# Seven products in six of eight up blocks, and thirteen whole units

## The chip, the core and the metric

The kernel runs on one core of a Trainium2 chip. TensorE (PE) multiplies, VectorE (DVE) and ScalarE (ACT) convert, scale and add, GpSimd (POOL) does a little elementwise work, and SyncE (SP) issues the loads. Each engine runs its own instructions in order, and semaphores tie them together. The metric is the time of one execution on the device in microseconds (us).

## The reference

A decoder trunk of two layers over 256 rows of 2048 columns, in float32. Each layer has an attention (differential in layer 0, latent in layer 1), a cross attention to 256 memory rows, and an MLP; each is normed before and added to the stream after. The change lies in the MLP:

```python
def sq_relu_mlp(h, wup, wdown):
    return jnp.square(jax.nn.relu(h @ wup)) @ wdown

x = x + sq_relu_mlp(rms_norm(x, mlp_norm[i]), mlp_wup[i], mlp_wdown[i])
```

with `wup` of 2048 x 8192 and `wdown` of 8192 x 2048 in each layer.

## The kernel before

**A product in three.** The kernel keeps float32 accuracy with operands of a shorter kind: every operand is held as a high half (rounded, type fp32r) and a low half (what rounding left), and one product is three matmuls, high by high, high by low, low by high. The activations are the stationary operand, 128x128, and the weights the moving one, 512 columns.

**A tile of weights.** `fetch` and `split_weights` load 1 MB of weights, 128 x 2048, into one of six tiles of the pool `wraw` (`raw`, line 168). `halves_of` makes from it two half tiles: for each, ScalarE casts 1024 columns into `whi` (line 193) and VectorE subtracts that from the raw tile into `wlo` (line 194). The pool `whalf` has four buffers of each, which is two tiles. `fill` keeps four tiles (`AHEAD`) prepared in the program's order ahead of the one that `take` hands to TensorE.

**The MLP in blocks.** The 8192 hidden columns are eight blocks of 1024. An *up block* multiplies the normed stream by one block of `wup`; its relu, squared and transposed, is kept in two *hidden units*, `hid[b, c]`, one for each half of 512 columns. A *down* group multiplies hidden units by the rows of `wdown` that belong to them, in four chunks of 512 output columns, and each chunk ends with two additions to the stream, one for each 128 rows (`add_residual`, line 428). An ordinary tile is one *item* of a line: 24 matmuls, for two row tiles.

**Seven products.** For the blocks in `SEVEN` the class `Seven` cuts the product of activations (2 x 2 parts: row tile by half of the inner dimension) and weights (2 x 2 parts) in the manner of Strassen and Winograd: seven products of sums and differences in place of eight. Each product takes two tiles (`x` 0 and 1) of 12 matmuls each into one bank, named `pr`, so a block has 14 items. The sums of the activations (`s1` to `s4`) are made once a layer. The sums of the weights are made for each block by VectorE in place, on whole raw tiles: for `p5` (line 735), `p7` (740), `p6` (743) and `p4` (748), each out of a newly loaded tile and a tile that is still kept, or of two kept ones. Twelve tiles are loaded for a block, where an ordinary block loads eight. `products` then adds the seven results: `p1` and `p5` are copied out of their banks by ScalarE (line 780), and after `p6`, `p2` and `p4` seven additions on VectorE (line 775) give the four quarters of the block. `out` takes each: relu and square on ScalarE (lines 1026 and 1027), transposes on TensorE (line 162), and a split into halves (lines 282 and 283).

**The order.** `mlp_line` writes out the order of items by hand. Before, it starts with up block 0, and then each of the blocks 1, 3, 5 and 7 is spread over the ordinary items of one group: the down group of the blocks that wait, and the next even up block. At the end comes the down group of block 7 alone. TensorE's instructions keep the program's order. Those of the other engines are put in order by a scheduler that runs its own picture of the time. A transpose is placed in TensorE's order when a running count of time in the program (`clock`) has passed the wait that its task named: `T_SQ + 2.0`, 6.4 us, for the results of the seven products.

**Units.** The pool `units` has twelve tiles of 8 KB in each partition, and beside them two half units of 4 KB, which the latent attention uses for its rotated queries. In the MLP, eight units hold the activations and their sums, and the others are hidden units.

Of the kernel before, what the change touches and what calls it, by code (L numbers as in the profile page):

```python
# [11 lines left out]
F32R = mybir.dt.float32r  # L12
# [5 lines left out]
P = 128  # L18
D = 2048
S = 256  # L20
NT = 2
CH = 512
# [1 line left out]
WARM = 16  # L24
RAWS = 6
MLP_BLOCKS = 8
SEVEN = (1, 3, 5, 7)
EVS = 7

T_EV, T_TURN, T_ROT, T_SM, T_SQ, T_ADD, T_NORM = 2.6, 2.6, 9.0, 6.5, 4.4, 2.2, 4.5  # L30
# [15 lines left out]
def trunk(ctx, tc, x, xT, mem, memT, positions, gcols, gfinal, lam_vecs, consts, W, out):  # L46
    nc = tc.nc

    def pool(name, bufs, space=None):
        kw = {"space": space} if space else {}  # L50
        return ctx.enter_context(tc.tile_pool(name=name, bufs=bufs, **kw))
# [1 line left out]
    keep = pool("keep", 1)  # L53
    wraw = pool("wraw", RAWS)
    whalf = pool("whalf", 4)
    units = pool("units", 12)
    work = pool("work", 2)
    small = pool("small", 3)
    banks = pool("banks", 8, bass.MemoryType.PSUM)
# [3 lines left out]
    def nm(s):  # L63
        serial[0] += 1
        return f"{s}_{serial[0]}"

    def unit():
        return units.tile([P, 2, 4, S], F32R, tag="unit", name=nm("unit"))

    def half_unit():  # L70
        return units.tile([P, 2, 2, S], F32R, tag="half", name=nm("half"), bufs=2)

    def bank(tag="ax"):
        return banks.tile([P, CH], F32, tag="bank", name=nm(tag))
# [7 lines left out]
    class Task:  # L82
        def __init__(self, gen):
            self.gen = gen
            self.done = False
            self.waits = None
            self.ready = clock[0]
            self.serial = serial[0]
            side.append(self)
            self.step()  # L90
# [36 lines left out]
    class Held:  # L127
# [6 lines left out]
        def run(self, gen):  # L134
            self.tasks.append(Task(gen))
            return self
# [7 lines left out]
    def side_bank():  # L144
        while not free_banks[0]:
            yield 0.5
        free_banks[0] -= 1
        return bank()

    def give_back():  # L150
        free_banks[0] += 1
# [45 lines left out]
    plan = []  # L197
# [492 lines left out]
        plan_k(f"ca_wo{l}", 4)  # L690

    def plan_mlp(l):
        plan.extend(j for item in mlp_lines[l] for j in item.jobs)

    class Chunk:


        def __init__(self, l, kind, blocks, c):
            self.kind, self.blocks, self.c = kind, blocks, c
            if kind == "up":  # L700
                self.all = [(f"mlp_wup{l}", 4 * (2 * blocks[0] + c) + u, CH) for u in range(4)]
            else:
                self.all = [(f"mlp_wdown{l}", 8 * b + 2 * c + u, CH) for b in blocks for u in range(2)]

        def items(self):
            return [Item(self, u, [job]) for u, job in enumerate(self.all)]
# [89 lines left out]
                out(1, 0, c["u3"])  # L796

    def mlp_line(l):
        def up(b):
            return [i for c in range(2) for i in Chunk(l, "up", [b], c).items()]  # L800

        def down(blocks):
            return [i for c in range(4) for i in Chunk(l, "down", blocks, c).items()]

        line = up(0)
        waiting = [0]
        for b in SEVEN:
            rest = down(waiting) + (up(b + 1) if b < 7 else [])
            seven = Seven(l, b).items()
            i = 0  # L810
            for k, item in enumerate(rest):
                while i < len(seven) and i * (len(rest) - 3) / len(seven) <= k:
                    line.append(seven[i])
                    i += 1
                line.append(item)
            waiting = [b, b + 1] if b < 7 else [b]
        return line + down(waiting)

    mlp_lines = {l: mlp_line(l) for l in range(2)}

# [113 lines left out]
    def keep2(rs, scale, tag):  # L934
        o = []
        for t in range(NT):
            k = small.tile([P, 1], F32, tag=tag, name=nm(tag), bufs=4)
            nc.vector.tensor_scalar(k, rs[t], scale, None, ALU.mult)
            o.append(k)
        return o  # L940
# [70 lines left out]
    def mlp(l, norm, gnext):  # L1011
        a = norm.done()
        rstd = keep2(norm.rstd, 1.0, "r1")
        hid = {}

        chunk = {}
        copied = {}

        def out(b, c, t, src, r, wait):

            if (b, c) not in hid:
                hid[b, c] = Held(unit())
            dst = hid[b, c]

            def task():
                nc.scalar.activation(r, src, AF.Relu, scale=rstd[t])
                nc.scalar.activation(r, r, AF.Square)
                yield wait
                pt = yield from side_bank()
                split(dst, t, transpose4(r, pt))  # L1030
                yield T_TURN
                give_back()

            dst.run(task())

        def finish_chunk(of, ps, nxt):
            for t in range(NT):
                if of.kind == "up":
                    r = work.tile([P, CH], F32, tag="ev", name=nm("ev"), bufs=EVS)
                    out(of.blocks[0], of.c, t, ps[t], r, T_SQ)  # L1040
                else:
                    add_residual(t, of.c, ps[t])
                    if nxt is not None:
                        nxt(of.c, t, ps[t])

        def acts_of(of):
            if of.kind == "up":
                return [a.unit_of(u) for u in range(4)]
            return [hid[b, c] for b in of.blocks for c in range(2)]

        def run(line, nxt=None):
            for item in line:
                of = item.of
                if isinstance(of, Seven):
                    of.products(
                        a, item.u, copied,
                        lambda t, c, r, b=of.b: out(b, c, t, r, r, T_SQ + 2.0),
                    )
                    continue
                n = len(of.all)  # L1060
                if nxt is not None and of.c == 3:
                    if item.u == 0:
                        finish_chunk(of, matmul_chunk(acts_of(of), turns=True), nxt)
                    continue
                if item.u == 0:
                    chunk["ps"] = [bank("mm") for _ in range(NT)]
                    chunk["acts"] = acts_of(of)
                act = chunk["acts"][item.u]
                need(act.tasks)
                for h, (hi, lo) in enumerate(take()):  # L1070
                    for t in range(NT):
                        unit_part(chunk["ps"][t], act, h, hi, lo, t, item.u == 0, item.u == n - 1)
                if item.u == n - 1:
                    finish_chunk(of, chunk["ps"], nxt)

        line = mlp_lines[l]
        tail = sum(len(i.of.all) == 2 and i.of.kind == "down" and i.of.blocks == [7] for i in line if not isinstance(i.of, Seven))
        limit = free_banks[0] - 1
        free_banks[0] -= limit
        run(line[:-tail])  # L1080

        def last(nxt):
            free_banks[0] += limit
            run(line[-tail:], nxt)

        if gnext is None:
            return last
        nxt = Stream(gnext)
        last(nxt.feed)
        return nxt  # L1090
# [31 lines left out]
    )  # L1122
    norm = cross(0, norm, m, mk)
    norm = mlp(0, norm, G_ATTN + 16)


# [32 lines left out]
    ps = matmul_chunk(acts, LAT)  # L1159
    latent_piece(eq, 0, ps, 0, LAT)  # L1160
    ps = matmul_chunk(acts, LAT)
# [4 lines left out]
    ps = matmul_chunk(acts, 320)  # L1166
# [24 lines left out]
        yield T_TURN  # L1191

    def project_latent(gi):
        qr, q, k, v = Held(half_unit()), Held(unit()), Held(unit()), unit()
        ps = matmul_chunk([cq], 256)

        def rotated(ps):
            es = []
            for t in range(NT):
                e = evacuate(ps[t][:, :256], rq[t])  # L1200
                rope(e[:, :256].rearrange("p (h d) -> p h d", h=4), cos[:, t, hd:], sin[:, t, hd:], 4, hm)
                es.append(e)
            yield T_ROT
            b = yield from side_bank()
            for t in range(NT):
                pt = b[:, 2 * t * P : 2 * (t + 1) * P]
                for i in range(2):
                    flip(pt[:, i * P : (i + 1) * P], es[t][:, i * P : (i + 1) * P])
            for t in range(NT):
                split(qr, t, b[:, 2 * t * P : 2 * (t + 1) * P].rearrange("p (k t) -> p k t", k=2))  # L1210
            give_back()
            yield T_TURN

        qr.run(rotated(ps))
        ps = matmul_chunk([cq])
        if gi == 0:
            krope.run(shared_key())
        for t in range(NT):
            heads_T(ps[t], t, rq[t], q, spare=True)
        ps = matmul_chunk([ckv])  # L1220
        for t in range(NT):
            heads_T(ps[t], t, rkv[t], k, spare=True)
        ps = matmul_chunk([ckv])
        for t in range(NT):
            values(ps[t], t, rkv[t], v)
        return qr, q, k, v
# [13 lines left out]
    down = mlp(1, norm, None)  # L1240
# [112 lines left out]
```

## Time and profile before

| | |
|---|---|
| median of 3 runs | 2284.94 us (2284.89 to 2284.94) |
| the profiled execution | 2284.52 us |
| its span, first to last instruction | 2282.7 us |
| granted TensorE clock, mean | 0.996 |
| TensorE busy | 2255.7 us, 99% |
| VectorE busy | 1609.0 us, 70% |
| ScalarE busy | 1281.1 us, 56% |
| 16 DMA engines busy, queue of SyncE | 56.9% |

A row of a group names line, engine, operation, output and inputs by the program's names, shape and count, then busy time, the mean of one in ns, the idle time ahead, and who ended it. A row of the timeline has start, length, engine, line and operation, and in brackets the wait ahead of it. `raw<-raw,raw` is a combination of weights, `wlo<-raw,whi` a split of half a tile. A matmul's listed length overlaps the next one.

### The profile page before, as it was taken

The numbers are of one execution on the slowest core, as the hardware profiler recorded it, in microseconds if no ns is written. First come the engines' busy times: TensorE is split into PE (matmuls) and PEld (weight loads), VectorE is DVE, ScalarE is ACT, GpSimd is POOL, SyncE is SP. The second block draws the span as 40 slices with busy tenths as digits, with TensorE's granted clock in tenths as the row PEclk, the third lists the DMA queues.
The fourth block names the chain that finished last, engine by engine and source line by source line (L and its number), as shares of the span: only waits on it lengthen the run. The fifth ranks groups of instructions, "written<-read, shape, count | busy, mean of one in ns | idle before, by whom it ended". The sixth has DMA issues, their size and how long they took to land.

```text
span 2282.7 us, 27403 instructions
## 1 busy us (share of the span) xinstructions
PE 2255.7 (99%) x10668; PEld 1884.4 (83%) x10668; DVE 1609.0 (70%) x1766; ACT 1281.1 (56%) x1731; POOL 103.4 (5%) x194
## 2 busy tenths in 40 slices
PE   8999999999999999999999999999999999999998
PEld 6888888888888888888889888888888888888886
DVE  5556657677877776777865666778787776777775
ACT  6554545566565465465555655566556546546564
POOL 0010110000000000000000311000000000000001
PEclk9999999999999999999999999999999999999999
DMA  9355555436666666666655344643766666666672
GB/s 358 121 175 187 196 203 190 166 124 226 234 228 229 220 209 226 224 204 237 223 178 174 124 142 148 240 148 129 255 243 204 220 221 221 221 221 209 233 258 74
DMA packets 69826, 458.90 MB, mean 201 GB/s; under 512 B 8001, under 2 KB 8129, under 8 KB 16961
## 3 DMA queue, kind: packets, MB, share of 16 engines
q1 hardware_dynamic: 69120, 456.12, 56.9%
q8 instruction: 83, 1.36, 0.2%
q10 hardware_dynamic: 576, 1.05, 0.2%
q14 instruction: 47, 0.38, 0.0%
HBM read 455.04 MB, written 2.10 MB: 200 GB/s over the span
## 4 chain that ended last, share of the span: by engine, by line
PE 96%; ACT 1%; DVE 1%; DMA 1%; POOL 0%; issue 0%; ACTq 0%; POOLq 0%; SPq 0%
PE mm L158 77%; PE pr L158 13%; PE ax L158 3%; PE ax L162 2%; PE mm L162 1%; ACT whi L193 1%; DMA raw<-in_da_wqkv_dram 0%; DVE wlo L194 0%; DMA raw<-in_memT_dram 0%; POOL rope L444 0%; POOL ev L449 0%; ACT junk L311 0%; ACT ev L433 0%; ACT p L490 0%; POOL rope L447 0%
## 5 line engine op out<-in xcount | busy, mean ns | idle before, releaser
L158 PE MATMUL mm<-whi,unit 128*128 128x512 f32 (+1 forms) x5312 | 1679.7, 389 | 1.4 <-ACT unit L561 0.9
L194 DVE TENSOR_TENSOR wlo<-raw,whi 128x1024 fp32r<-128x1024 f32 (+2 forms) x890 | 1071.6, 1212 | 560.1 <-ACT whi L193 541.1
L193 ACT CAST whi<-raw 128x1024 fp32r<-128x1024 f32 (+2 forms) x890 | 926.1, 1041 | 850.8 <-PE mm L158 763.2
L158 PEld LDWEIGHTS mm<-whi,unit 128*128 128x128 f32 x5312 | 994.5, 188 | 198.2 <-ACT unit L561 1.3
L158 PE MATMUL mm<-wlo,unit 128*128 128x512 f32 (+1 forms) x2656 | 1026.1, 386 | 0.8 <-DVE wlo L194 0.8
L158 PEld LDWEIGHTS mm<-wlo,unit 128*128 128x128 f32 x2656 | 500.3, 188 | 95.6 <-DVE wlo L194 1.4
L158 PE MATMUL pr<-whi,unit 128*128 128x512 f32 x896 | 298.0, 391 | 0.0
L158 PEld LDWEIGHTS pr<-whi,unit 128*128 128x128 f32 x896 | 168.3, 188 | 34.6
L158 PE MATMUL pr<-wlo,unit 128*128 128x512 f32 x448 | 174.4, 389 | 0.0
L428 DVE TENSOR_TENSOR x<-x,mm 128x512 f32<-128x512 f32 x160 | 105.2, 681 | 7.7 <-PE mm L158 6.7
L158 PEld LDWEIGHTS pr<-wlo,unit 128*128 128x128 f32 x448 | 84.1, 188 | 16.9
L317 POOL TENSOR_TENSOR rs<-rs,mhalf 128x1 f32<-128x1 f32 (+1 forms) x28 | 23.6, 846 | 1278.8 <-DVE rs L316 1278.8
L283 DVE TENSOR_TENSOR unit<-ax,unit 128x512 fp32r<-128x512 f32 x80 | 54.0, 684 | 1.1
L282 ACT CAST unit<-ax 128x512 fp32r<-128x512 f32 x80 | 45.6, 581 | 13.4 <-PE ax L162 13.4
L490 ACT ACTIVATE p<-ax,nmax 128x256 f32<-128x256 f32 (+1 forms) x80 | 33.6, 427 | 27.2 <-DVE nmax L488 26.1
L743 DVE TENSOR_TENSOR raw<-raw,raw 128x2048 f32<-128x2048 f32 x16 | 36.6, 2290 | 10.0 <-DMA raw<-in_mlp_wup_dram 9.8
L311 ACT ACTIVATE junk<-x 128x512 bf16<-128x512 f32 x56 | 35.2, 628 | 9.4 <-DVE x L428 8.4
L1251 POOL TENSOR_TENSOR x<-x,unit 128x512 f32<-128x512 f32 x6 | 8.9, 1502 | 668.2 <-ACT junk L311 668.2
L735 DVE TENSOR_TENSOR raw<-raw,raw 128x2048 f32<-128x2048 f32 x16 | 36.6, 2286 | 3.3 <-DMA raw<-in_mlp_wup_dram 2.6
L740 DVE TENSOR_TENSOR raw<-raw,raw 128x2048 f32<-128x2048 f32 x16 | 36.6, 2288 | 3.2 <-DMA raw<-in_mlp_wup_dram 3.0
L158 PE MATMUL ax<-unit,unit 128*128 128x256 f32 (+1 forms) x240 | 37.2, 281 | 0.0
L748 DVE TENSOR_TENSOR raw<-raw,raw 128x2048 f32<-128x2048 f32 x16 | 36.7, 2292 | 0.5
(148 smaller groups left out, 1009.7 us busy)
## 6 DMA issues: line engine op xcount, KB each, us to landing
raw<-in_mlp_wup_dram SPq DMA_DIRECT2D x160, 1024.0 KB, 5.0
raw<-in_mlp_wdown_dram SPq DMA_DIRECT2D x128, 1024.0 KB, 4.9
raw<-in_da_wqkv_dram SPq DMA_DIRECT2D x47, 1024.0 KB, 5.0
raw<-in_da_wo_dram SPq DMA_DIRECT2D x16, 1024.0 KB, 4.9
raw<-in_ca_wkv_dram SPq DMA_DIRECT2D x16, 1024.0 KB, 5.0
raw<-in_mla_wo_dram SPq DMA_DIRECT2D x16, 1024.0 KB, 5.1
raw<-in_ca_wq_dram SPq DMA_DIRECT2D x8, 1024.0 KB, 4.9
raw<-in_ca_wo_dram SPq DMA_DIRECT2D x8, 1024.0 KB, 4.9
```

Source lines behind the costliest of these rows:

```text
L158: return nc.tensor.matmul(o, stationary, moving, start=start, stop=stop)
L162: nc.tensor.transpose(o, src, ident)
L193: nc.scalar.copy(hi, r)
L194: nc.vector.tensor_tensor(lo, r, f32(hi), ALU.subtract)
L282: nc.scalar.copy(hi, src)
L283: nc.vector.tensor_tensor(dst[:, 1, :n, t * P : (t + 1) * P], src, f32(hi), ALU.subtract)
L311: nc.scalar.activation(junk[:, : src.shape[1]], src, AF.Square, accum_out=acc)
L428: nc.vector.tensor_tensor(xc, xc, ps, ALU.add)
L735: nc.vector.tensor_tensor(o, o, r.pop("11"), ALU.subtract)
L740: nc.vector.tensor_tensor(o, r.pop("22"), o, ALU.subtract)
L743: nc.vector.tensor_tensor(o, r.pop("t3"), o, ALU.add)
L748: nc.vector.tensor_tensor(o, o, r.pop("21"), ALU.subtract)
```

## The change

Six of the eight up blocks of a layer, 1, 2, 3, 5, 6 and 7, are multiplied by seven products, in place of 1, 3, 5 and 7. The ordinary up blocks are 0 and 4. Block 0 comes first as before. All other ordinary items but the last down group form one list, in which block 4 comes in two halves of 512 columns, (4, 0) and (4, 1), each of which joins the down group of a block ahead of it: the down groups are 0; 1 with (4, 0); 2; 3 with (4, 1); 5; 6; and 7 at the end. Over this list the 84 items of the six blocks are spread evenly. A `Chunk` is therefore given pairs of block and half in place of blocks, and `mlp_line` returns the line and its end. The pool has 13 units, and the rotated queries use half of a whole unit.

```diff
-SEVEN = (1, 3, 5, 7)
+SEVEN = (1, 2, 3, 5, 6, 7)
...
-    units = pool("units", 12)
+    units = pool("units", 13)
...
-    def half_unit():
-        return units.tile([P, 2, 2, S], F32R, tag="half", name=nm("half"), bufs=2)
...
     def plan_mlp(l):
-        plan.extend(j for item in mlp_lines[l] for j in item.jobs)
+        plan.extend(j for line in mlp_lines[l] for item in line for j in item.jobs)
...
-        def __init__(self, l, kind, blocks, c):
-            self.kind, self.blocks, self.c = kind, blocks, c
+        def __init__(self, l, kind, halves, c=0):
+            self.kind, self.halves, self.c = kind, halves, c
             if kind == "up":
-                self.all = [(f"mlp_wup{l}", 4 * (2 * blocks[0] + c) + u, CH) for u in range(4)]
+                ((b, h),) = halves
+                self.all = [(f"mlp_wup{l}", 4 * (2 * b + h) + u, CH) for u in range(4)]
             else:
-                self.all = [(f"mlp_wdown{l}", 8 * b + 2 * c + u, CH) for b in blocks for u in range(2)]
+                self.all = [(f"mlp_wdown{l}", 8 * b + 2 * c + h, CH) for b, h in halves]
...
     def mlp_line(l):
-        def up(b):
-            return [i for c in range(2) for i in Chunk(l, "up", [b], c).items()]
-
-        def down(blocks):
-            return [i for c in range(4) for i in Chunk(l, "down", blocks, c).items()]
-
-        line = up(0)
-        waiting = [0]
-        for b in SEVEN:
-            rest = down(waiting) + (up(b + 1) if b < 7 else [])
-            seven = Seven(l, b).items()
-            i = 0
-            for k, item in enumerate(rest):
-                while i < len(seven) and i * (len(rest) - 3) / len(seven) <= k:
-                    line.append(seven[i])
-                    i += 1
-                line.append(item)
-            waiting = [b, b + 1] if b < 7 else [b]
-        return line + down(waiting)
+        def up(b, h):
+            return Chunk(l, "up", [(b, h)]).items()
+
+        def down(*halves):
+            return [i for c in range(4) for i in Chunk(l, "down", halves, c).items()]
+
+        def both(b):
+            return (b, 0), (b, 1)
+
+        line = up(0, 0) + up(0, 1)
+        rest = (
+            down(*both(0)) + up(4, 0) + down(*both(1), (4, 0)) + down(*both(2))
+            + up(4, 1) + down(*both(3), (4, 1)) + down(*both(5)) + down(*both(6))
+        )
+        seven = [i for b in SEVEN for i in Seven(l, b).items()]
+        i = 0
+        for k, item in enumerate(rest):
+            while i < len(seven) and i * (len(rest) - 3) / len(seven) <= k:
+                line.append(seven[i])
+                i += 1
+            line.append(item)
+        return line, down(*both(7))
...
-            return [hid[b, c] for b in of.blocks for c in range(2)]
+            return [hid[k] for k in of.halves]
...
-        qr, q, k, v = Held(half_unit()), Held(unit()), Held(unit()), unit()
+        qr, q, k, v = Held(unit()[:, :, :2]), Held(unit()), Held(unit()), unit()
```

The lines after the change are up to ten lower or higher by number: the combinations are 733, 738, 741 and 746, the split 191, the load 165, the residual addition 425.

More of the change, by code (lines that the diff above doesn't have):

```diff
@@ L1039, in finish_chunk @@
                     r = work.tile([P, CH], F32, tag="ev", name=nm("ev"), bufs=EVS)
-                    out(of.blocks[0], of.c, t, ps[t], r, T_SQ)
+                    out(*of.halves[0], t, ps[t], r, T_SQ)
                 else:
@@ L1074, in run @@
                     finish_chunk(of, chunk["ps"], nxt)
-        line = mlp_lines[l]
-        tail = sum(len(i.of.all) == 2 and i.of.kind == "down" and i.of.blocks == [7] for i in line if not isinstance(i.of, Seven))
+        line, end = mlp_lines[l]
         limit = free_banks[0] - 1
         free_banks[0] -= limit
-        run(line[:-tail])
+        run(line)
         def last(nxt):
             free_banks[0] += limit
-            run(line[-tail:], nxt)
+            run(end, nxt)
         if gnext is None:
```

## The prediction

> **What bounds the kernel now.** I read the page's busy shares first, then the chain that ended last, then TensorE's waits, and then the two stretches in which blocks are multiplied by seven products, because the shares are an average over stages.
>
> ```profile
> span 2282.7 us, 27403 instructions
> PE 2255.7 (99%) x10668; PEld 1884.4 (83%) x10668; DVE 1609.0 (70%) x1766; ACT 1281.1 (56%) x1731; POOL 103.4 (5%) x194
> ...
> PE 96%; ACT 1%; DVE 1%; DMA 1%; POOL 0%; issue 0%; ACTq 0%; POOLq 0%; SPq 0%
> ...
> 714.56 10.88 PE mm L158 x48
> ```
>
> The chain is TensorE from end to end. In it 48 matmuls of 128x512 take 10.88 us, so one costs 0.2267 us when nothing holds it up. The 389 ns of the group list is a length that overlaps the next one.
>
> ```profile
> 559.00:1145.00 586.00, 585.34 (x2638) 484.24 (x2637) 438.74 (x382) 330.88 (x360) 0.00 (x0) 1.00 0.64 224
> 1645.00:2230.00 585.00, 584.34 (x2630) 483.18 (x2629) 434.81 (x380) 328.01 (x356) 0.00 (x0) 1.00 0.64 224
> 576.00:658.00 82.00, 82.00 (x363) 67.90 (x362) 67.67 (x59) 44.33 (x44) 0.00 (x0) 1.00 0.65 231
> ```
>
> The columns are the length, then the busy time of PE, PEld, DVE, ACT and POOL, the clock, the DMA share and GB/s. The first two rows are the seven-product stages of the two layers, the third is the densest piece of the first, with one item of the seven products to one ordinary item. TensorE never rests; VectorE is busy 75% of a stage, 83% of the dense piece.
>
> ```profile
> PE ax L162 <- ACT u L1027: 1.3, 2, 0.7
> ...
> DVE wlo L194 <- ACT whi L193: 129.4, 114, 1.5
> ACT whi L193 <- PE mm L158: 211.4, 137, 1.7
> DVE raw L743 <- DMA raw<-in_mlp_wup_dram: 5.5, 4, 2.1
> ```
>
> Waits in all, their number, the longest. The first row is of the whole run and is TensorE's only wait within these stages; the rest are of the first stage. VectorE's idle time is mostly back pressure: four buffers of split weights (two tiles) are full, ScalarE waits for TensorE to empty one, VectorE for ScalarE. A little of it is not: a combination of weights that stands waiting for its load.
>
> **The change, part by part.** *Fewer matmuls.* An ordinary block costs 2 column halves x 4 units x 24 = 192 matmuls, a block by seven products 7 x 2 x 12 = 168. Four more blocks in the two layers go over: 4 x 24 = 96 fewer, which the program's own order confirms (10,668 to 10,572). 96 x 0.2267 = 21.8 us, 10.9 a layer, all on the chain. A stage shrinks from 586 to 575.1 us.
>
> *More for VectorE.* Per layer: 24 more half-tile splits (12 tiles), 16 combinations, 14 additions of products, and 16 residual additions, since the order has seven down groups of four chunks in place of five. Their prices:
>
> ```profile
> 633.54 5.76 DVE L194 TENSOR_TENSOR wlo<-raw,whi 128x1024 fp32r<-128x1024 f32 x5
> ...
> 545.64 2.29 DVE L735 TENSOR_TENSOR raw<-raw,raw 128x2048 f32<-128x2048 f32 x1 [0.70 <-DVE unit L283]
> 547.85 1.22 DVE L194 TENSOR_TENSOR wlo<-raw,whi 128x1024 fp32r<-128x1024 f32 x1
> ...
> 576.12 1.28 DVE L428 TENSOR_TENSOR x<-x,mm 128x512 f32<-128x512 f32 x2
> ```
>
> Back to back a split costs 5.76 / 5 = 1.15, a combination 547.85 - 545.64 = 2.21, a 512-column addition 0.64. So 24 x 1.15 + 16 x 2.21 + 30 x 0.64 = 82.2 us a layer, and VectorE has 438.7 + 82.2 = 520.9 us in 575.1: 91%. Its cover is TensorE, with 54 us left a layer.
>
> *More for ScalarE:* 24 casts and 4 copies of products.
>
> ```profile
> L193 ACT CAST whi<-raw 128x1024 fp32r<-128x1024 f32 x266 | 280.4, 1054 | 246.4 <-PE mm L158 211.4 <-PE pr L158 27.4 <-DVE wlo L194 7.0
> L780 ACT COPY p<-pr 128x512 f32<-128x512 f32 x8 | 4.6, 574 | 0.0
> ```
>
> 24 x 1.054 + 4 x 0.574 = 27.6, and 358 of 575 us is 62%: hidden.
>
> *More loads.* 12 a block in place of 8, so 8 more of 1 MB a layer; 224 GB/s become about 243, and bytes do not bind (the page's first slice moved 358 GB/s). What binds is when a load can start. All six raw tiles are always taken, so each load waits for the VectorE instruction that frees one.
>
> ```profile
> DMA to landing us min/median/max: 4.7/5.0/7.4
> ...
> 624.43 0.33 SPq L168 DMA_DIRECT2D raw<-in_mlp_wup_dram  x1
> ...
> 631.33 2.29 DVE L743 TENSOR_TENSOR raw<-raw,raw 128x2048 f32<-128x2048 f32 x1 [2.09 <-DMA raw<-in_mlp_wup_dram]
> 633.54 2.35 DVE L194 TENSOR_TENSOR wlo<-raw,whi 128x1024 fp32r<-128x1024 f32 x2
> 635.11 0.39 PE L158 MATMUL pr<-wlo,unit 128*128 128x512 f32 x1
> ```
>
> The first row is of the first stage's loads of up weights. The others are one wait: the load starts at 624.43, VectorE stands 2.09 us until 631.33, and the split behind the combination (an earlier tile's; it only stands behind it in the queue) ends at 633.54 + 1.22 = 634.76. TensorE takes it at 635.11, 0.35 us later. The kernel before is this near its edge. In the instruction order of both programs I added up VectorE's work between the instruction that frees a raw tile and the combination that reads the new load. Before, 48 of 96 such loads in the two layers have under 5.0 us of work to hide in, together 43.0 us short per layer; after, 52 of 144, together 32.0. The new order is longer, not tighter, because more of VectorE's work lies between; but before, the shortfall fell into 147 us of idle time per layer, and now into 54.
>
> *Bursts.* At the end of a block the product additions crowd in. VectorE's order there (W split of half a tile, C combination, a product addition, s split of activations):
>
> ```
> before: a W a a W a a W a W s W s W W s W a
> after:  a W a W a C W a a W s a W W s W W s a
> ```
>
> Both hold 8 W, four tiles, for which TensorE has 2 x 5.44 + 2 x 2.72 = 16.3 us of matmuls (24 and 12 x 0.2267) and about 1.6 of transposes. VectorE needs 8 x 1.15 + 10 x 0.64 = 15.6 before and 2.2 more, 17.8, after. A lead lost ahead of this piece isn't won back in it.
>
> To price lateness I carried these sums along VectorE's order, TensorE at its unstalled pace: a split not before the half four ahead is used up and ScalarE's 1.05 us are over, a combination not before its load landed. The order before then has no split late, as in the trace. The new one has splits late at six or seven places a layer: 3.2 us in all with landings of 5.0, 4.7 with 5.2, 10.9 with 5.6. Each lateness may also shift what follows and so help the next place; the largest alone is 1.8. I take 4.7, since the rows have a tail (7.4) behind the median; the ends are 1.8 and 10.9.
>
> *Transposes behind the additions.* TensorE's order puts the first transposes of a finished block 30 matmuls, 6.8 us, after the sixth product, as before.
>
> ```profile
> 816.10 0.68 DVE L775 TENSOR_TENSOR u<-pr,p 128x512 f32<-128x512 f32 x1
> ...
> 818.55 0.69 DVE L775 TENSOR_TENSOR u<-pr,p 128x512 f32<-128x512 f32 x1
> ...
> 820.04 0.63 ACT L1027 ACTIVATE u<-u 128x512 f32<-128x512 f32 x1
> ...
> 821.84 0.60 PE L162 MATMUL ax<-identr,u 128*128 128x128 f32 x4
> ```
>
> ScalarE is done at 820.67, 1.17 us early, after three additions with one split among them. In the new order four of six blocks a layer have two splits there: 1.15 more, margin nil; the sixth block has two residual additions besides, 1.28 late; a combination ahead of the second output costs up to 1.2 in two blocks. Together 0 to 5 us a layer, and partly the same lateness as above; I take 2.5.
>
> *Units.* Thirteen units and no half units fill the same memory. Beside eight units of activations and their sums, five are left, and the new order never holds more than five hidden units. Outside the MLP the engines' orders are unchanged, and no unit's first write waits for TensorE beyond its own transposes: nothing, either way.
>
> *The sum.* The profiled execution took 2284.52 us, 0.42 under the median of the runs, 2284.94. 2284.94 - 21.8 + 2 x (4.7 + 2.5) = 2277.5.
>
> *A rule weighed.* Five splits in a row take 5.76 us, 1.15 each, where the list has 1.22 to 1.23 for one: the end of one overlaps the start of the next. The Trainium skill, "VectorE: DVE Perf Modes", section on the TRN2 errata, says that a fixed latency is paid between instructions, and that an fp32 tensor_tensor takes (N+151)/0.96 ns, 1224 for a split. This trace agrees with the length of one and not with paying all of it in a row. By the page's formula VectorE's stage would come to an estimated 554 us in place of 521, and the kernel to about the time before (the third rival has the same mechanism from rows).
>
> **The rivals.** *Nothing stalls* (2263 to 2267): VectorE's 521 us fit into 575 and the order spreads them. For it: no late split before, and fewer short loads per combination. Against it: margins of 0.35 and 1.17 that the bursts use up. 0.15.
>
> *Slower, by the raw tiles.* VectorE waits behind a combination whose load has just started, loses its lead of two tiles, and TensorE stops at most blocks. With landings of 6.0 my sums make 19.4 us late a layer, and with 2.5 for transposes 21.9: 2284.9 - 21.8 + 43.8 = 2307. It decides from 13.2 us of stops a layer (10.9 and half of 4.6), which landings of about 5.7 bring. Against it the median of 5.0; for it the 2.09 us wait. Most of this case would lie near 2292. 0.21.
>
> *VectorE is the bound.* If its instructions overlapped no longer once it is nearly full, a stage would cost their listed lengths: 296 splits x 1.22 + 48 combinations x 2.29 + 118 additions x 0.68 = 551 us, and with the 32 of waits 583, 8 more than TensorE's 575. That leaves 2.9 of the 10.9, and with 2.5 for transposes 0.4 a layer: 2284. Against it the five splits in a row. 0.07.
>
> *The clock falls.* A stop of 7 us early in the run shows what a long one costs:
>
> ```profile
> 54.20:58.00 3.80, 3.11 (x11) 2.52 (x12) 0.92 (x2) 1.17 (x2) 1.67 (x6) 0.50 0.01 2
> 58.00:62.00 4.00, 4.00 (x14) 3.18 (x14) 0.47 (x1) 0.59 (x1) 0.00 (x0) 0.72 0.02 4
> ```
>
> 3.8 x 0.5 + 4.0 x 0.28 = 3.0 us more per such stop. My stops are under 2 us, so this comes only with the slower rival. The Trainium skill, "TensorE: Matmul & The Clock Gate", section "HAM oscillation", puts the limit at idle gaps of about 3.4 us; these rows agree that 7 us is beyond it, and none here shows a gap near the limit. 0.02 by itself.
>
> *The change does nothing* has no place: the matmuls are gone from the order.
>
> **How the numbers follow.** My forecast, part of the saving kept, has 0.55 with 2267 to 2283 as its own range. Under 0.2% (4.6 us) a measurement of this kernel tells little from no change: below 2280.4 is faster, above 2289.5 slower. Faster is nine tenths of my case and the first rival, 0.50 + 0.15 = 0.65; same is the rest of mine, the third rival and the fourth, 0.14; slower 0.21. The range leaves out the far end of the slower rival and the lowest of the first: 2264 to 2292.
>
> **What would show it.** Right: the seven-product stages near 575 us plus 3 to 11 each, VectorE near 521 us in each, TensorE waits of 0.2 to 2 us for splits and for the transposes' inputs, most of them at block ends, attention unchanged. Wrong: TensorE waits of over 3 us, a clock under 1.00 in the stages, or landings of over 5.5 us at the combinations; or no waits at all.

## The result, and the profile after

The changed kernel takes 2296.84 us (median of four runs, 2294.0 to 2302.2) against 2284.91 of the kernel before beside it: ratio 1.0056, 95% interval 1.004 to 1.0072. It is slower by 0.56%; 2277.5 was forecast, and the range ended at 2292. The profiled execution is the longest of the four, 2302.2 us with a span of 2300.4; that of before had 2284.52 and 2282.7. So the profile has 17.7 us to explain where the medians differ by 11.9. The mean granted clock of the four runs was 0.992, 0.993, 0.995 and 0.995 at 2302.2, 2299.2, 2294.4 and 2294.0 us, so the profiled run is also the one that lost most by the clock.

The page of the changed kernel, its span, the busy shares and the engines' shares of the chain that ended last:

```profile
span 2300.4 us, 27468 instructions
PE 2248.5 (98%) x10572; PEld 1871.0 (81%) x10572; DVE 1760.1 (77%) x1906; ACT 1337.6 (58%) x1787; POOL 103.4 (4%) x194
...
PE 87%; DVE 6%; DMA 2%; ACT 2%; issue 2%; POOL 0%; ACTq 0%; POOLq 0%; SPq 0%; DVEq 0%
```

The 96 matmuls are gone, and TensorE no longer carries 96% of the chain but 87%; VectorE, ScalarE and loads stand in it. Where that happens is read from the first and last product matmul of each layer's stage, first after, then before:

```profile
L155 PE MATMUL pr<-whi,unit x672: 388/389/776, 559.9 to 1154.4; 128*128 128x512 f32 x168
...
L155 PE MATMUL pr<-whi,unit x672: 388/389/775, 1638.1 to 2230.8; 128*128 128x512 f32 x168
```

```profile
L158 PE MATMUL pr<-whi,unit x448: 388/389/481, 559.1 to 1144.9; 128*128 128x512 f32 x150
...
L158 PE MATMUL pr<-whi,unit x448: 388/389/481, 1627.0 to 2213.1; 128*128 128x512 f32 x150
```

The stages last 594.5 and 592.7 us in place of 585.8 and 586.1: 8.7 and 6.6 more, where 10.9 less was due from the matmuls. The other 2.4 lie outside the stages. Of the same two stretches that the prediction shows of before (PE, PEld, DVE, ACT and POOL busy, clock, DMA share, GB/s), the changed kernel has

```profile
559.00:1145.00 586.00, 571.74 (x2551) 469.60 (x2550) 508.76 (x446) 353.45 (x381) 0.00 (x0) 1.00 0.66 237
1645.00:2230.00 585.00, 572.65 (x2553) 470.24 (x2552) 506.66 (x446) 352.66 (x380) 0.00 (x0) 0.99 0.65 236
```

TensorE stands still for 14 and 12 us in each, with VectorE at 87%: it has 77 us left over and is late all the same. What TensorE waits for in the first stage and then in the second (us in all, times, longest):

```profile
PE ax L159 <- ACT u L1031: 8.7, 4, 2.7
PE pr L155 <- DVE wlo L191: 3.2, 4, 1.7
PE mm L155 <- DVE wlo L191: 1.7, 1, 1.7
PE ax L159 <- ACT p L1031: 0.7, 2, 0.4
```

```profile
PE ax L159 <- ACT u L1031: 8.7, 4, 2.7
PE mm L155 <- DVE wlo L191: 2.1, 2, 1.7
PE pr L155 <- DVE wlo L191: 1.1, 2, 0.7
PE ax L159 <- ACT p L1031: 0.3, 1, 0.3
```

VectorE's own waits for loads, whole run:

```profile
DVE raw L741 <- DMA raw<-in_mlp_wup_dram: 18.6, 14, 2.2
DVE raw L738 <- DMA raw<-in_mlp_wup_dram: 11.1, 8, 2.0
DVE raw L733 <- DMA raw<-in_mlp_wup_dram: 4.5, 5, 1.5
```

They add up to 34 us; in the kernel before such waits are 15.4 us in the whole run. Of TensorE's waits, the first rows are the transposes of a finished block's output: before, this wait was 1.3 us in the whole run. The end of block 1 shows where it comes from. First the kernel before, in a block of its first stage: the last matmul of the sixth product and what VectorE runs next.

```profile
814.81 0.39 PE L158 MATMUL pr<-whi,unit 128*128 128x512 f32 x1
...
813.60 2.59 DVE L194 TENSOR_TENSOR wlo<-raw,whi 128x1024 fp32r<-128x1024 f32 x2 [0.75 <-ACT whi L193]
```

The product ends at 815.20, and VectorE begins with the additions at 816.10, 0.90 later. In the changed kernel, from the timeline (start, length, engine, instruction, in brackets the wait ahead of it):

```profile
639.79 0.39 PE L155 MATMUL pr<-whi,unit 128*128 128x512 f32 x1
...
649.40 0.66 PE L159 MATMUL ax<-identr,u 128*128 128x128 f32 x4 [2.42 <-ACT u L1031]
...
638.37 2.28 DVE L746 TENSOR_TENSOR raw<-raw,raw 128x2048 f32<-128x2048 f32 x1
640.57 2.35 DVE L191 TENSOR_TENSOR wlo<-raw,whi 128x1024 fp32r<-128x1024 f32 x2
642.85 0.68 DVE L773 TENSOR_TENSOR u<-pr,p 128x512 f32<-128x512 f32 x1
643.45 1.21 DVE L191 TENSOR_TENSOR wlo<-raw,whi 128x1024 fp32r<-128x1024 f32 x1
...
646.32 0.68 DVE L773 TENSOR_TENSOR u<-pr,p 128x512 f32<-128x512 f32 x1
...
647.02 1.04 ACT L190 CAST whi<-raw 128x1024 fp32r<-128x1024 f32 x1 [0.30 <-DVE u L773]
...
648.72 0.63 ACT L1031 ACTIVATE u<-u 128x512 f32<-128x512 f32 x1
```

The sixth product ends at 640.18. VectorE is then in p4's combination, with two splits behind it in its queue, and comes to the first addition at 642.85, 2.67 after the product. The third addition ends at 647.00, 4.15 after the first began (before: 819.24 - 816.10 = 3.14, one split fewer). ScalarE has a cast ahead of its two steps and is done at 649.35, 2.35 after that addition (before 820.67 - 819.24 = 1.43). Together 1.77 + 1.01 + 0.92 = 3.70 us later than before, against the margin of 1.17 that the prediction read: 2.5, and the wait is 2.42. TensorE's order still has these transposes 30 matmuls behind the sixth product.

That is one block. The same three pieces in every block, from the timeline (us, rounded; the two layers agree to 0.01):

| block | first addition behind the product | from there to the end of the third | ScalarE done behind that | wait |
|---|---|---|---|---|
| before, 1 | 0.91 | 3.14 | 3.35 | 0.66 |
| before, 3, 5 and 7 | 0.91 | 3.14 | 1.42 | none |
| after, 1 | 2.66 | 4.15 | 2.35 | 2.42 |
| after, 2 | 0.91 | 4.75 | 2.76 | 1.68 |
| after, 3 and 6 | 0.91 | 3.14 | 1.42 | none |
| after, 5 | 1.04 | 4.63 | 2.94 | 1.87 |
| after, 7 | 2.66 | 5.35 | 1.42 | 2.69 |

The first addition is late in blocks 1 and 7 alone, where p4's combination stands right ahead of it. Against 0.91, 3.14 and 1.42 the four blocks that wait are later by 3.6 us in all at the first addition, by 6.3 between the additions, and by 3.8 at ScalarE, where casts or the steps of another output stand ahead. Four margins of 1.17 take 4.7 off these 13.8.

The second cost is the clock. The same wait at the end of block 7, the last of the six, and what follows it:

```profile
1140.75 1.12 PE L159 MATMUL ax<-identr,u 128*128 128x128 f32 x4 [2.69 <-ACT u L1031]
1141.52 0.78 PE L155 MATMUL pr<-whi,unit 128*128 128x512 f32 x1
...
1147.05 0.40 PE L155 MATMUL mm<-wlo,unit 128*128 128x512 f32 x1
```

```profile
1142.00:1143.00 1.00, 1.00 (x4) 0.71 (x3) 1.00 (x3) 1.00 (x2) 0.00 (x0) 0.50 0.89 328
1727.00:1731.00 4.00, 3.57 (x12) 2.99 (x13) 4.00 (x6) 1.03 (x3) 0.00 (x0) 0.57 0.38 104
2218.00:2222.00 4.00, 3.60 (x11) 3.01 (x12) 3.04 (x6) 1.60 (x4) 0.00 (x0) 0.58 0.76 248
```

The granted clock is 0.50 after the wait, until about 1147: 13 matmuls take 5.53 us from 1141.52 to 1147.05 instead of 13 x 0.2267 = 2.95, and the four transposes ahead of them 0.77 instead of 0.41 (block 1's), so 2.9 more. The last two rows are the second layer: the clock fell after block 1's wait of 2.42, which ends at 1727.43, and after block 7's of 2.69, which ends at 2218.41, for about 3.4 us each; that is 1.5 and 1.7 more on the same count. Block 1's wait of 2.42 in the first layer, ending at 649.40, was followed by full clock. A further fall, at 1283 to 1287 in the attention, comes after a wait of 2.1 us for GpSimd that the kernel before has too. In that kernel's profiled run the clock held there, but it fell at the same place in two runs below that are the kernel before with one small edit (0.51 over 1273 to 1276 with later transposes, 0.50 over 1272 to 1275 with thirteen units), so it needs none of the new products. Of the 2.4 us outside the stages 1.6 lie between the two, and 3.4 us at half the clock are 1.7; the 0.8 ahead of the first stage are not followed.

The sum of the first layer: -10.9 of matmuls, + 9.4 of transposes (8.7 + 0.7), + 4.9 of splits, + 2.9 of clock make + 6.3; measured is + 8.7. Of the second: -10.9 + 9.0 + 3.2 + 3.2 = + 4.5, measured + 6.6. A wait is listed from the modelled end of the matmul ahead, 0.39 after its start, where the next one would have started after 0.23: that is 0.16 more for each of 11 and 9 waits, 1.8 and 1.4. The kernel before had a wait of 0.8 on this count in each stage, which comes off. About 1.5 us a layer are left, and most of that is in stops too short for a row: matmuls with no listed wait between them start 0.2286 and 0.2288 apart on the mean, in place of 0.2281 and 0.2282, over some 2,420.

### The profile page after: what moved, and what is told of

It reads as the page before. It is cut to its first block, busy times and chain, and to the rows that moved or that the text cites. A ratio compares the mean times of both kernels' runs of the same rounds, so it can differ in the third digit from the quotient of the medians.

```text
span 2300.4 us, 27468 instructions
## 1 busy us (share of the span) xinstructions
PE 2248.5 (98%) x10572; PEld 1871.0 (81%) x10572; DVE 1760.1 (77%) x1906; ACT 1337.6 (58%) x1787; POOL 103.4 (4%) x194
## 4 chain that ended last, share of the span: by engine, by line
PE 87%; DVE 6%; DMA 2%; ACT 2%; issue 2%; POOL 0%; ACTq 0%; POOLq 0%; SPq 0%; DVEq 0%
PE mm L155 65%; PE pr L155 16%; DVE wlo L191 3%; PE ax L155 3%; PE ax L159 2%; DMA raw<-in_mlp_wup_dram 2%; ACT whi L190 1%; PE mm L159 1%; DVE x L425 1%; DMA raw<-in_da_wqkv_dram 0%; DVE raw L738 0%; DVE raw L746 0%; DVE u L773 0%; DVE p L773 0%; DVE raw L741 0%
## 5 line engine op out<-in xcount | busy, mean ns | idle before, releaser
L155 PE MATMUL mm<-whi,unit 128*128 128x512 f32 (+2 forms) x4800 | 1523.0, 390 | 0.9 <-ACT unit L558 0.9
L190 ACT CAST whi<-raw 128x1024 fp32r<-128x1024 f32 (+3 forms) x938 | 976.6, 1042 | 809.2 <-PE mm L155 673.5
L191 DVE TENSOR_TENSOR wlo<-raw,whi 128x1024 fp32r<-128x1024 f32 (+3 forms) x938 | 1121.5, 1211 | 410.3 <-ACT whi L190 389.7
L155 PEld LDWEIGHTS mm<-whi,unit 128*128 128x128 f32 x4800 | 900.4, 189 | 178.6 <-ACT unit L558 1.3
L155 PE MATMUL mm<-wlo,unit 128*128 128x512 f32 (+2 forms) x2400 | 928.3, 387 | 4.6 <-DVE wlo L191 4.5
L155 PE MATMUL pr<-whi,unit 128*128 128x512 f32 x1344 | 443.4, 393 | 0.0
L155 PEld LDWEIGHTS pr<-whi,unit 128*128 128x128 f32 x1344 | 254.1, 189 | 52.1
L155 PE MATMUL pr<-wlo,unit 128*128 128x512 f32 x672 | 264.1, 393 | 4.5 <-DVE wlo L191 4.3
L425 DVE TENSOR_TENSOR x<-x,mm 128x512 f32<-128x512 f32 x192 | 126.3, 681 | 10.3 <-PE mm L155 9.3
L741 DVE TENSOR_TENSOR raw<-raw,raw 128x2048 f32<-128x2048 f32 x24 | 54.9, 2289 | 18.8 <-DMA raw<-in_mlp_wup_dram 18.6
L738 DVE TENSOR_TENSOR raw<-raw,raw 128x2048 f32<-128x2048 f32 x24 | 54.9, 2288 | 11.2 <-DMA raw<-in_mlp_wup_dram 11.1
L733 DVE TENSOR_TENSOR raw<-raw,raw 128x2048 f32<-128x2048 f32 x24 | 54.9, 2286 | 5.2 <-DMA raw<-in_mlp_wup_dram 4.5
L280 DVE TENSOR_TENSOR unit<-ax,unit 128x512 fp32r<-128x512 f32 (+1 forms) x88 | 57.1, 659 | 0.5 <-ACT unit L279 0.3
L746 DVE TENSOR_TENSOR raw<-raw,raw 128x2048 f32<-128x2048 f32 x24 | 55.0, 2290 | 0.6
```

The lines of the kernel that those rows point to most:

```text
L155: return nc.tensor.matmul(o, stationary, moving, start=start, stop=stop)
L190: nc.scalar.copy(hi, r)
L191: nc.vector.tensor_tensor(lo, r, f32(hi), ALU.subtract)
L280: nc.vector.tensor_tensor(dst[:, 1, :n, t * P : (t + 1) * P], src, f32(hi), ALU.subtract)
L425: nc.vector.tensor_tensor(xc, xc, ps, ALU.add)
L733: nc.vector.tensor_tensor(o, o, r.pop("11"), ALU.subtract)
```

## Experiments

Three theories stood against each other. *Theory 1:* VectorE reaches a block's additions without its lead, and TensorE's transposes, at a fixed distance behind the sixth product, come too early for it; put later, they find their input ready. *Theory 2:* VectorE has no time left at all, so that a stop taken away at one place comes back at another. *Theory 3:* the loads of the combinations are what makes VectorE late.

**The transposes later** (in the changed kernel, the hidden block's due time in `run()`):

```
-    lambda t, c, r, b=of.b: out(b, c, t, r, r, T_SQ + 2.0),
+    lambda t, c, r, b=of.b: out(b, c, t, r, r, T_SQ + 5.0),
```

> The changed kernel with one number changed: the transposes of the seven products' results are placed 3 us later in TensorE's order (T_SQ + 5.0 in place of T_SQ + 2.0). Theory 1 (VectorE reaches the additions late at block ends, and TensorE stands at a transpose that was placed too early): the 18 us of waits for ScalarE's u and p go, the two falls of the clock behind them too, and the time comes to 2274 to 2281. Theory 2 (VectorE has no time left at all, so a stop merely moves): the waits come back in front of the splits, 2290 to 2297. Theory 3 (loads of combinations): little change, 2288 to 2297.

2277.96 us (2276.94 to 2281.33), 0.9969 of before, 0.9957 to 0.9981: faster than both kernels. The waits of the whole run and the first stage:

```profile
PE ax L159 <- ACT u L1031: 3.2, 4, 1.1
...
PE mm L155 <- DVE wlo L191: 4.5, 4, 1.7
...
PE pr L155 <- DVE wlo L191: 2.6, 5, 0.8
```

```profile
559.00:1145.00 586.00, 581.14 (x2605) 477.68 (x2604) 516.40 (x455) 359.13 (x390) 0.00 (x0) 1.00 0.66 240
```

The transposes' waits fall from 17.3 to 3.2 us (8.7 + 8.7 are 17.3 before rounding), the splits' from 8.8 to 7.1, and no stage shows a clock under 1.00. VectorE has the same work and does more of it in the same 586 us. A stop that VectorE's lack of time made would have moved to the splits; it went. This speaks for theory 1 and against theory 2.

**The combinations left out** (each load is made, the weights go into the products as they are):

```
-    nc.vector.tensor_tensor(o, o, r.pop("11"), ALU.subtract)
+    r.pop("11")
...
-    nc.vector.tensor_tensor(o, o, r.pop("21"), ALU.subtract)
+    r.pop("21")
```

> The changed kernel without the four combinations of weights (the loads and everything else stay; the blocks by seven products are therefore computed with uncombined weights). VectorE has 53 us less a layer, and no instruction of it stands in its queue for a load of its own. Theories 1, 2 and 3 all expect the stops in the stages to go: 2263 to 2270. If it stays above 2280, the cause is none of them but the order of matmuls itself or the units.

2265.26 us, 0.9917 (0.9902 to 0.9931).

```profile
559.00:1145.00 586.00, 584.32 (x2634) 483.53 (x2633) 427.96 (x412) 363.81 (x396) 0.00 (x0) 1.00 0.68 242
```

TensorE rests 1.7 us in the stretch, and the time is 2 us over the full saving, 2284.9 - 21.8 = 2263.1. So the matmuls give what was counted for them, and all of the loss hangs on VectorE's combinations, by their time or by their place.

**p4's combination alone left out**, the one that stands ahead of the first addition:

```
-    nc.vector.tensor_tensor(o, o, r.pop("21"), ALU.subtract)
+    r.pop("21")
```

> The changed kernel with one combination left out, the one for p4, which stands in VectorE's queue just ahead of a block's first product addition (the fourth product is computed with uncombined weights; loads, splits and TensorE's order are the same). Theory 1 (VectorE comes to the additions of a block with its lead gone): 26 us less for VectorE, all of it ahead of the additions, so the 18 us of waits at the transposes fall under 6 and the time to 2270 to 2280. Theory 3 (loads): the waits for loads at the other three combinations stay near 34 us, and with them the stops, 2288 to 2297.

2278.5 us, 0.9971 (0.996 to 0.9982).

```profile
PE ax L159 <- ACT u L1031: 3.4, 2, 1.7
...
DVE raw L741 <- DMA raw<-in_mlp_wup_dram: 16.0, 12, 2.2
DVE raw L738 <- DMA raw<-in_mlp_wup_dram: 7.4, 7, 1.7
```

The first addition starts 0.91 us after the product in every block, in blocks 1, 5 and 7 too, and the transposes' waits fall to 3.4, while VectorE still stands 28 us for loads (16.0, 7.4 and 4.6 at L733) where it stood 34 in the changed kernel. Waiting for loads does not carry the loss. Taking out this one combination does away with it, but with it 26 us of VectorE's work a layer go, and five of six blocks now have one split between the additions; no run left out another combination alone, so this run by itself does not part the place from the work. Block 2, whose first addition was never late, keeps its wait of 1.68 in both layers.

**No loads behind three combinations** (p5, p7 and p6 are made from a kept tile, with the same work for VectorE):

```
-    o = self.fetch(0, 1, x)
-    nc.vector.tensor_tensor(o, o, r.pop("11"), ALU.subtract)
+    o, a = raw_tile(), r.pop("11")
+    nc.vector.tensor_tensor(o, a, a, ALU.add)
```

> The changed kernel in which the combinations for p5, p7 and p6 make their tile from the kept one alone (same size and engine, wrong weights), so that these three load nothing: six loads a block in place of twelve. VectorE's work is the same. Theory 3 (VectorE standing at a combination for its load): the 34 us of such waits go, and with them most stops, 2268 to 2278. Theory 1 and 2 (VectorE's own work): the waits at the transposes stay at over 12 us, 2286 to 2297.

2339.52 us, 1.0242 (1.0225 to 1.0259): much slower, and outside what any of the theories had expected. The loads' waits went from 34 to 4.6 us and the splits' of products to 1.3, but

```profile
PE ax L159 <- ACT u L1033: 47.7, 12, 5.4
```

```profile
639.83 0.68 DVE L775 TENSOR_TENSOR u<-pr,p 128x512 f32<-128x512 f32 x1
...
641.56 2.29 DVE L733 TENSOR_TENSOR raw<-raw 128x2048 f32<-128x2048 f32 x1
...
646.64 0.69 DVE L775 TENSOR_TENSOR u<-pr,p 128x512 f32<-128x512 f32 x1
```

Without a load to wait for, VectorE's order has the next block's first combination between the first and the third addition (block 1, shown), which lie 6.8 us apart in place of 3.5, or directly ahead of the first, which then starts 3.11 us after the product (blocks 2, 3 and 6). So this run changed the place of a combination as well as the loads, and as a whole it is no clean test of theory 3. Block 7 is one: VectorE's order there is as in the changed kernel, and with nearly all of the loads' waits gone the first addition still comes 2.66 us after the product, the third ends 5.35 after that one began, and TensorE waits 2.69. With the run before it theory 3 falls. The rest shows theory 1 at a higher dose.

**p4's combination on GpSimd**, to unload VectorE:

```
-    nc.vector.tensor_tensor(o, o, r.pop("21"), ALU.subtract)
+    nc.gpsimd.tensor_tensor(o, o, r.pop("21"), ALU.subtract)
```

> The changed kernel with the combination for p4 on GpSimd in place of VectorE (same result). It is the one that stands right ahead of a block's first product addition. Theory 1: the addition comes up to 2.2 us earlier in eight of twelve blocks, the transposes' waits fall from 18 us to under 6, 2280 to 2286. Theory 2: VectorE gains 26 us a layer and the waits for splits fall as well, under 2280. Theory 3: no change from 2297, since p4's combination waits for no late load. A combination takes about 6 us on GpSimd (1.5 us for 512 columns in the row of the last norm), which could make p4's split late: then waits for splits of p4 rise.

2329.39 us, 1.0188 (1.0173 to 1.0204); each theory had expected 2297 or less.

```profile
PE mm L155 <- DVE wlo L191: 19.5, 14, 2.5
PE pr L155 <- DVE wlo L191: 18.6, 18, 2.0
```

```profile
639.00 5.72 POOL L746 TENSOR_TENSOR raw<-raw,raw 128x2048 f32<-128x2048 f32 x1 [31.49 <-DVE wlo L191]
...
640.36 5.43 DVE L191 TENSOR_TENSOR wlo<-raw,whi 128x1024 fp32r<-128x1024 f32 x1
```

The combination costs 5.72 us there (4.70 as a mean of 24; 2.28 on VectorE), and VectorE doesn't go on beside it: the split that starts at 640.36 takes 5.43 us in place of 1.22 and ends at 645.79, 1.07 after GpSimd's end at 644.72, so it is held until GpSimd is done. The longest split of the run is 5.66. So nothing is unloaded, and now TensorE waits 38 us for splits.

**The dose.** With the transposes still later, T_SQ + 7.0:

```
-    lambda t, c, r, b=of.b: out(b, c, t, r, r, T_SQ + 2.0),
+    lambda t, c, r, b=of.b: out(b, c, t, r, r, T_SQ + 7.0),
```

> The changed kernel with the transposes 5 us later than it has them (T_SQ + 7.0). With 3 us later 3.2 us of waits for u were left and 7.1 for splits. If the rest of the transposes' waits is lateness too, 2274 to 2278; the waits for splits should stay at 6 to 9 us, since nothing of VectorE's work is changed. If results held longer in the seven ev buffers become the limit, it is slower than 2278.

2277.53 us, 0.9967 (0.9955 to 0.9979). There is no wait for `u` left, but

```profile
PE mm L155 <- DVE wlo L191: 8.1, 7, 2.1
PE pr L155 <- DVE wlo L191: 4.9, 7, 1.2
```

13.0 us of waits for splits in place of 7.1, where 6 to 9 had been expected. From +2.0 over +5.0 to +7.0 the kernel takes 2296.8, 2278.0 and 2277.5: past +5.0 a stop does move, as theory 2 says of all of it.

**The same edit in the kernel before** (T_SQ + 5.0), a control:

```
-    lambda t, c, r, b=of.b: out(b, c, t, r, r, T_SQ + 2.0),
+    lambda t, c, r, b=of.b: out(b, c, t, r, r, T_SQ + 5.0),
```

> A control: the kernel before with the transposes of the seven products' results 3 us later (T_SQ + 5.0). If late transposes are worth something only where VectorE is late, nothing is to be had here beyond the 1.3 us that TensorE waits for u: 2283.5 to 2285.5. If the place of the transposes were worth as much by itself, it would fall to 2270 or so and the gain in the changed kernel would not be a part of the change's cost.

2285.15 us, 0.9998 (0.9989 to 1.0008). Later transposes give nothing where they waited only 1.3 us in all, so the gain above is the repair of what the change broke.

**The kernel before with its transposes earlier** (T_SQ - 1.0, 3 us sooner), to make the fault without the change:

```
-    lambda t, c, r, b=of.b: out(b, c, t, r, r, T_SQ + 2.0),
+    lambda t, c, r, b=of.b: out(b, c, t, r, r, T_SQ - 1.0),
```

> The kernel before with the transposes of the seven products' results 3 us earlier (T_SQ - 1.0). The first transpose of a block had 1.17 us to spare in six of eight blocks and none in two. If a transpose ahead of its data is what costs the changed kernel its time, the same must show here with VectorE's load unchanged: about 8 x 2 = 16 us of waits for ScalarE's u, each of them near 2 us, and some falls of the clock after them: 2298 to 2308, the waits for splits still under 1 us. If waits at transposes are harmless by themselves (another stop takes their place), it stays under 2290.

2298.6 us, 1.006 (1.0045 to 1.0075).

```profile
PE ax L162 <- ACT u L1027: 13.5, 8, 2.4
```

A loss and a wait like those of the changed kernel stand there with VectorE's work unchanged: 13.5 us of waits, and 13.1 on the time (2285.5 beside it). In the stages the clock fell once, to 0.83 over 1730 to 1740, after a wait of 2.43. VectorE's load is not needed for such a loss; the distance between producer and transposes is enough.

**The kernel before with thirteen units**, the rotated queries in half of a whole one:

```
-    units = pool("units", 12)
+    units = pool("units", 13)
...
-    qr, q, k, v = Held(half_unit()), Held(unit()), Held(unit()), unit()
+    qr, q, k, v = Held(unit()[:, :, :2]), Held(unit()), Held(unit()), unit()
```

> One part of the change alone: the kernel before with 13 units, the rotated queries in half of a whole unit, and the order of blocks as before. All theories: no difference, 2284 to 2286, the attention's waits as before. A difference of over 2 us would give the units a share in the result.

2285.14 us, 0.9999 (0.999 to 1.0008): the part of the change that touches memory costs nothing.

**An attempt at more**: T_SQ + 5.0, and the product p2 ahead of p6, its output in a tile of its own.

```
-    ORDER = ("p1", "p5"), ("p3", "p7", "p6", "p2", "p4")
+    ORDER = ("p1", "p5"), ("p3", "p7", "p2", "p6", "p4")
...
```

> The changed kernel with transposes 3 us later, and the second product taken ahead of the sixth, so that the two combinations that wait for loads most (p7, p6) no longer follow each other and fewer additions crowd at one place; its result goes into a tile of its own. What is left there are about 7 us of waits for splits and 34 us of VectorE's waits for loads. If those come from p7's and p6's combinations standing next to each other, both fall and the time is 2270 to 2276. If they come from VectorE's load as a whole, it stays at 2276 to 2280. With one more ev tile held, it could be slower.

2285.06 us, 0.9994 (0.9984 to 1.0004): a miss.

```profile
PE ax L159 <- ACT u L1032: 5.9, 8, 1.7
...
PE pr L155 <- DVE wlo L191: 5.2, 5, 1.3
```

It waits more at both places than the run with later transposes alone (for `u` 2.7 us more; for splits 2.2 more, 9.3 with 4.1 at `mm`) and is no better than the kernel before. That is 4.9 of the 7.1 us between the two. In its profiled run, the slowest of ten (2280.8 to 2288.1), the clock also fell to 0.50 over 583 to 586, after a wait of 2.08 for a split. The rest was not followed.

**What stays open.** With later transposes the changed kernel is still some 15 us above 2263, the full saving. 10.3 of them are the listed waits for splits (7.1) and for `u` (3.2), of which the kernel before has 2.1 itself. Most of the rest is the 0.16 that each of these waits costs beyond its row, some 2 us, and stops too short for a row, some 4: matmuls without a listed wait start 0.2290 apart in the stages in place of 0.2282, over 4,880. Without combinations nearly all of it goes (first stage: 1.7 in all for `u`). Which order of combinations and splits would spare them was tried once and not found.

## Why the prediction was wrong

- *Fewer matmuls: right.* 96 fewer, and 2265.26 us without combinations against the full saving's 2263.1.
- *VectorE's load: right in size.* 521 us a stage forecast; 509 and 507 in the shown stretches, 516 in that with later transposes. It is not the bound (the third rival): with the same load the kernel takes 2278.0 with later transposes.
- *Splits late, 4.7 us a layer: right.* 4.9 and 3.2 measured, at five and four places, the longest 1.7. The loads landed after 4.9 us as a median (longest 8.1).
- *Transposes behind the additions, 2.5 us a layer: the step that failed.* Measured 9.4 and 9.0, also beyond the stated end of 5. The step counted only what stands between the additions: one split more in four blocks, "margin nil", and 1.28 in the sixth, 5.9 us a layer in all. That was right; 6.3 were measured. But it left the first addition at 0.90 us after the product, and ScalarE's part at 1.43. In blocks 1 and 7 the first addition came 2.66 after it, 3.6 us a layer, and in blocks 1, 2 and 5 ScalarE was later by 3.8 us a layer; with the margin already used up, both went into the wait. The order written out in the prediction begins with the first addition, so p4's combination and the two splits ahead of it are not in it; its "C" is the next block's first combination. The sentence beside it says that a lead lost ahead of this piece is not won back, and the transposes' term did not take it up. ScalarE's share could be read before: in block 1 of each layer of the kernel before its casts make it 3.35 instead of 1.42, and that is the 1.3 us of waits for `u` that the prediction shows.
- *The clock: wrong in its condition.* It was to come only with the slower rival, as stops were to stay under 2 us. Three stops, of 2.69, 2.42 and 2.69 us, were followed by a fall, and the falls took 2.9, 1.5 and 1.7 more. Nor would a stop under 2 us have been safe: in the kernel before itself, ahead of the MLP, a wait of 1.75 us goes with a clock of 0.50.

```profile
378.37 1.08 PE L162 MATMUL ax<-identr,os 128*128 128x128 f32 x4 [1.75 <-DVE os L648]
...
378.00:381.00 3.00, 2.63 (x9) 2.27 (x10) 1.05 (x3) 0.78 (x2) 0.00 (x0) 0.50 0.56 183
```

The Trainium skill, "TensorE: Matmul & The Clock Gate", section "HAM oscillation", puts the limit at idle gaps of about 3.4 us; here gaps of 2.69, 2.42 and 1.75 were followed by a clock of 0.50 and another of 2.42 was not, so the measurement decides: a gap well under that can be enough, and its length alone does not tell.

- *Units: right*, 0.9999.
- *The slower rival (0.21) had the right sign and nearly the time (most of it was put near 2292), but the wrong mechanism; that it came near is luck.* It priced late loads and combinations standing behind them. VectorE did wait for loads, 34 us in the run, but with 28 of them left the loss was gone once p4's combination was out of the way, and that one waits for no load.
- *The signs named:* waits at block ends for the transposes' inputs came as said, up to 2.69 us instead of 0.2 to 2. The stages took 575.1 and 19.4 or 17.6 more, where 3 to 11 were named. The sign for wrong, a clock under 1.00 in the stages, came; waits over 3 us did not.

## What to carry to other kernels

Where instructions of one engine are placed by hand at a fixed distance behind another engine's work, a change that loads the engine between them must be priced by when that engine *arrives* at the work, with all that stands ahead of it in its queue and in the queue of the next engine, not by the work in between alone, and not by its mean load (here 87% with 77 us to spare). If the arrival moves, move the placed instructions too: +3 us on one due time turned a loss of 0.56% into a gain of 0.31%. A wait of only 2.4 to 2.7 us cost 1.5 to 2.9 us more through the clock in three cases of four.

## What the runs showed of the hardware

A two-input GpSimd operation in SBUF did not run beside VectorE's two-input splits but held them: it took 4.70 us as a mean of 24, up to 5.72, and splits of 1.22 us were stretched to as much as 5.66. The Trainium skill, "Trainium Architecture — The Big Picture", section "What this means for kernel authors", says that the two engines share a port pair and that it is an exclusive lock; this trace agrees, since the split that was held at 640.36 ended 1.07 us after GpSimd's operation, about the 1.22 that a split takes alone.
